# Five weight pairs, three raw buffers, ten product buffers and two units split earlier in a macaron decoder trunk

## The chip, the cores and the metric

The kernel runs on one core of a Trainium2 chip. The metric is the device time of one execution in microseconds (us). The engines are PE (matmul), DVE (vector), ACT (scalar), POOL (GpSimd) and SP, which issues the weight loads. Each works through its own instructions in the order in which they stand, and they wait for each other on semaphores.

## What is computed

A decoder trunk of two layers for a sequence of 256 tokens of width 1024, in float32. Each layer is a half-weighted SwiGLU feed-forward block (FFN), a mixer and a second FFN. The mixer of layer 0 is a convolution, that of layer 1 an attention.

```python
def swiglu_ffn(x, w_gate_up, w_down):
    gate, up = jnp.split(x @ w_gate_up, 2, axis=-1)
    return (jax.nn.silu(gate) * up) @ w_down

def conv_mixers(h, w_in, a_kernel, b_kernel, b_bias, b_ln_g, b_ln_b, w_out):
    z = h @ w_in
    a_b, a_c, a_x, b_val, b_gate = jnp.split(z, [512, 1024, 1536, 2048], axis=-1)
    y_a = a_b * causal_depthwise_conv(a_c * a_x, a_kernel)          # 3 taps
    u = b_val * jax.nn.sigmoid(b_gate)
    u = causal_depthwise_conv(u, b_kernel) + b_bias                 # 31 taps
    y_b = jax.nn.silu(layer_norm(u, b_ln_g, b_ln_b))
    return jnp.concatenate([y_a, y_b], axis=-1) @ w_out
...
    for layer in range(2):
        x = x + 0.5 * swiglu_ffn(rms_norm(x, ffn1_norm[layer]), ffn1_w_gate_up[layer], ffn1_w_down[layer])
        h = rms_norm(x, mix_norm[layer])
        x = x + (conv_mixers(h, ...) if layer % 2 == 0 else dilated_attention(h, ...))
        x = x + 0.5 * swiglu_ffn(rms_norm(x, ffn2_norm[layer]), ffn2_w_gate_up[layer], ffn2_w_down[layer])
    return rms_norm(x, final_norm)
```

## The kernel before

Activations lie transposed in SBUF, 128 features by 256 tokens, as eight tiles. All weights come as one stream of 162 **units** of 1 MB (16 tiles of 128x128): units 0 to 21 are gate and up of the first FFN, 22 to 32 its down projection, 33 to 42 the ten pairs of the convolution's input projection, 43 to 46 its output projection, 47 to 79 the second FFN, and 80 to 161 layer 1 in the same way. SP loads unit by unit into the pool `raws`. `split` then writes a unit as two rounded halves, `w1` (a copy on ACT, line 127) and `w2` (the rest, a subtraction on DVE, line 128), each in two pieces of 1024 columns, or in four of 512 for the units in `FINE` (39, 46 and 47). PE multiplies with both halves (lines 163 to 165, or 169 and 170). The units in `whole` (0, 35, 42, 43 and 44) are not split: PE multiplies with the raw tile (line 161), and they keep their raw buffer until that is done.

`advance(u, ahead)` says how far the stream must be by unit `u`: units below `u + RAWS + WS - 1` are loaded, those below `u + ahead` split. `RAWS` is 4, `WS`, the number of buffers of `w1` and of `w2`, is 4 too, and `ahead` is `WS` unless it is given. In the convolution the table `AHEAD` gives it for each of the ten input units, `OUT_AHEAD` for units 43 and 44. A scheduler sets the final order on each engine from the order in the code and from priorities: `high_priority` puts a part of the code ahead of what stands before it, as for the layer norm of the convolution (`PRIO_LN`).

The convolution's stage, `conv`, is where the change works most. For each of four channel groups `c`, the 31 taps are shared: DVE adds its own into a PSUM tile (line 464), and for the others ACT multiplies (`prod`, line 486) and POOL adds (`yp`, line 487), 55 such adds in all. The products go through a pool of `PBUFS` = 18 buffers. `PER_STEP` and `PER_POOL` spread the taps over the ten units. The short convolution (`m`, then `ya`: ACT starts each group at line 518, DVE goes on at line 527) is gated by the last two units at lines 538 and 539. The sum over all channels for the layer norm goes through `sums` (line 561) into a matmul with ones (line 563), while PE multiplies the `ya` half with units 43 and 44. The normalised half, `ob`, then meets units 45 and 46; from their result come `x` (line 420) and the next block's `xs` (lines 190 and 191).

PSUM banks `pa` are four. DVE's reads at lines 382 and 340 set them free in an FFN.

Of the kernel before, what the change touches and what calls it, by code (L numbers as in the profile page):

```python
# [33 lines left out]
UT = 16  # L34
# [3 lines left out]
PER_STEP = [9, 8, 7, 8, 8, 8, 9, 8, 9, 10]  # L38
PRIO = 0
WHOLE = {9, 2}  # L40
PBUFS = 18
PER_POOL = [6, 8, 2, 6, 6, 9, 6, 4, 8, 9]
XPRIO = 0
AHEAD = [2, 4, 1, 1, 4, 4, 3, 4, 3, 3]
LATE = 15
OUT_AHEAD = [2, 3]
PRIO_LN = 800
# [18 lines left out]
M_POOL = [0, 0, 0, 0]  # L66
T_POOL = [0, 0, 0, 0]
B_POOL = [0, 0]
RAWS = 4
WS = 4  # L70
TWO = (3,)
ROBIN = False
SU_POOL = 2
# [21 lines left out]
def trunk(ctx: ExitStack, tc: tile.TileContext, xin, wst, cst, bia, idn, out):  # L95
    nc = tc.nc
    keep = ctx.enter_context(tc.tile_pool(name="keep", bufs=1))
    keep.tile([P, (LINE - BASE % LINE) // 4], F32, name="gap")
    raws = ctx.enter_context(tc.tile_pool(name="raws", bufs=RAWS))
    w1s = ctx.enter_context(tc.tile_pool(name="w1s", bufs=WS))  # L100
    w2s = ctx.enter_context(tc.tile_pool(name="w2s", bufs=WS))
    tmp = ctx.enter_context(tc.tile_pool(name="tmp", bufs=2))
# [4 lines left out]
    n_units = wst.shape[0]  # L107
    ahead_load, ahead_split = RAWS + WS - 1, WS
    raw, w1, w2 = {}, {}, {}
    at = {"load": 0, "split": 0}  # L110

    def load(u):
        raw[u] = raws.tile([P, UT * P], F32, name="raw")
        n = UT * P // PIECES.get(u, 1)
        for c in range(0, UT * P, n):
            nc.sync.dma_start(raw[u][:, c:c + n], wst[u][:, c:c + n])

    def split(u):
        if u in whole:
            return  # L120
        w1[u] = w1s.tile([P, UT * P], F32R, name="w1")
        w2[u] = w2s.tile([P, UT * P], F32R, name="w2")
        n = max(2, PIECES.get(u, 1), FINE.get(u - first_conv, 1))
        h = UT * P // n
        for i in range(n):
            c = slice(i * h, (i + 1) * h)
            nc.scalar.copy(w1[u][:, c], raw[u][:, c])  # L127
            nc.vector.tensor_sub(w2[u][:, c], raw[u][:, c], w1[u][:, c].bitcast(F32))  # L128
        del raw[u]

    def advance(u, ahead_split=ahead_split):
        while at["load"] < min(n_units, u + ahead_load):
            load(at["load"])
            at["load"] += 1
        while at["split"] < min(n_units, u + ahead_split):
            split(at["split"])
            at["split"] += 1


    first_conv = NF + NF * ND // UT  # L140
# [13 lines left out]
    def take(n):  # L154
        st = Stream(used[0])
        used[0] += n
        return st

    def mm3(o, a, b, start, stop, check=False):
        if len(a) == 1:  # L160
            nc.tensor.matmul(o, a[0], b[-1], start=start, stop=stop, skip_group_check=check)  # L161
            return
        nc.tensor.matmul(o, a[0], b[0], start=start, stop=False, skip_group_check=check)  # L163
        nc.tensor.matmul(o, a[0], b[1], start=False, stop=False, skip_group_check=check)  # L164
        nc.tensor.matmul(o, a[1], b[0], start=False, stop=stop, skip_group_check=check)  # L165

    def mm2(o, w, b, start, stop):

        nc.tensor.matmul(o, w[0], b, start=start, stop=False, skip_group_check=True)  # L169
        nc.tensor.matmul(o[:, 0], w[1], b[:, 0], start=False, stop=stop, skip_group_check=True)  # L170
# [13 lines left out]
    def split_to(o1, o2, src, scale=None):  # L184

        if scale is None:
            nc.scalar.copy(o1, src)
            nc.vector.tensor_sub(o2, src, o1.bitcast(F32))
        else:
            nc.scalar.activation(o1, src, AF.Copy, scale=scale)  # L190
            nc.vector.scalar_tensor_tensor(o2, src, scale, o1.bitcast(F32),  # L191
                                           op0=ALU.mult, op1=ALU.subtract)
# [119 lines left out]
    def twice(r):  # L312
        return r[:, None, :].to_broadcast([P, 2, S])

    def project(st, base, xs, xg=None):

        bank = psa.tile([P, 2, S], F32, name="pa")
        for i in range(2):
            for k in range(ND):
                w = st.tile(base + 2 * k + i)  # L320
                b = (xs[:, k, 0], xs[:, k, 1]) if len(w) == 2 else (xg[:, k],)
                mm3(bank[:, i], w, b, k == 0, k == ND - 1)
        return bank

    def project2(st, base, xs):

        banks = []
        for i in range(2):
            bank = psa.tile([P, 2, S], F32, name="pa")
            for k in range(ND):  # L330
                mm2(bank, st.tile(base + 2 * k + i), xs[:, k], k == 0, k == ND - 1)
            banks.append(bank)
        return banks

    def join(v, banks, r):

        for i, bank in enumerate(banks):
            h = tmp.tile([P, S], F32, name="sq")
            nc.scalar.copy(h, bank[:, 1])  # L339
            nc.vector.tensor_add(v[:, i], bank[:, 0], h)  # L340
        nc.vector.tensor_mul(v, v, twice(r))  # L341
# [23 lines left out]
    def ffn(norm, after, between=None, first=None):  # L365
        _, r = norm.end(True, first is None)
        with tc.tile_pool(name="gp", bufs=1, reuse_waits="tile") as gp:
            st = take(NF)
            start = GS_START[st.u // FFN_STEP] // 4
            gs = gp.tile([P, NF * 2 * S + start], F32R, name="gs")[:, start:].rearrange(  # L370
                "p (f t s) -> p f t s", f=NF, t=2)
            for p in range(NF):
                advance(st.u + p)
                one = p < ONES[st.u // FFN_STEP] or p >= NF - ONE_END
                if one:
                    bank = first if first and p == 0 else project(st, p * UT, norm.xs)
                else:
                    banks = project2(st, p * UT, norm.xs)
                with tc.high_priority(offset=PRIO_F):
                    v = tmp.tile([P, 2, S], F32, name="v")  # L380
                    if one:
                        nc.vector.tensor_mul(v, bank, twice(r))
                    else:
                        join(v, banks, r)
                    sl = tmp.tile([P, S], F32, name="sl")
                    nc.scalar.activation(sl, v[:, 0], AF.Silu)  # L386
                    g = tmp.tile([P, S], F32, name="g")
                    nc.vector.tensor_mul(g, sl, v[:, 1])
                    split_to(gs[:, p, 0], gs[:, p, 1], g)
            if between:  # L390
                between(gs[:, NF - 1, 0, :1].bitcast(F32))
            st = take(NF * ND // UT)
            for d in range(ND):
                acc = psb.tile([P, 2, S], F32, name="pb")
                two = d < ND - 1
                for f in range(NF):
                    t = d * NF + f
                    if t % UT == 0 or f == 0:
                        advance(st.u + t // UT)
                    if two:  # L400
                        mm2(acc, st.tile(t), gs[:, f], f == 0, f == NF - 1)
                    else:
                        mm3(acc[:, 0], st.tile(t), (gs[:, f, 0], gs[:, f, 1]), f == 0, f == NF - 1)
                for i in range(2 if two else 1):
                    nc.vector.scalar_tensor_tensor(x[:, d], acc[:, i], 0.5, x[:, d],  # L405
                                                   op0=ALU.mult, op1=ALU.add)
                after.add(d)
# [15 lines left out]
    def conv(norm, after):  # L423
        with tc.tile_pool(name="cp", bufs=1, reuse_waits="tile") as cp, \
                tc.tile_pool(name="cp2", bufs=PBUFS, reuse_waits="tile") as cp2:
            xg = cp.tile([P, ND, S], F32, name="xg")
# [65 lines left out]
            for p in range(10):  # L492
                advance(st.u + p, AHEAD[p])
                bank = project(st, p * UT, norm.xs, xg)
# [225 lines left out]
    for layer in range(DEPTH):  # L720
        nxt = Norm(C_MX + layer * ND, start=XS_START["MX"][layer])
        if layer == 0:
            ffn_first(norm, nxt)
        else:
            ffn(norm, nxt)
        norm, nxt = nxt, Norm(C_F2 + layer * ND, start=XS_START["F2"][layer])
        (conv if layer % 2 == 0 else attention)(norm, nxt)
        if layer < DEPTH - 1:
            norm, nxt = nxt, Norm(C_F1 + (layer + 1) * ND, start=XS_START["F1"][layer + 1])
            ffn(norm, nxt)  # L730
            norm = nxt
    with tc.tile_pool(name="fp", bufs=1, reuse_waits="tile") as fp:
# [4 lines left out]
        last = Norm(C_FN, y)  # L737
# [97 lines left out]
```

## Time and profile before

| what | us |
|---|---|
| median of three runs | 969.8 |
| lowest and highest run | 968.5 and 969.87 |
| the profiled execution, its own time | 970.47 |
| its span, first to last instruction | 968.7 |
| PE busy | 953.3 |
| DVE busy | 738.5 |
| ACT busy | 557.8 |
| POOL busy, all within the convolution and just behind it | 47.9 |

The profiled execution lies 0.7 us above the median. A busy time says how long an engine had an instruction at work; matmuls are pipelined, so two neighbours overlap in the records. Where a row ends with a bracket, it gives the idle time of the engine just before and what ended it. Times are counted from the span's start.

### The profile page before, as it was taken

To read this page: it belongs to the slowest core of one execution; us is meant where nothing else is said; L and a number is where in the kernel's file an instruction comes from. 1 tells how busy PE (TensorE), PEld (TensorE's weight loads), DVE (VectorE), ACT (ScalarE), POOL (GpSimd) and SP (SyncE) were. 2 spreads that over 40 slices of the span, in tenths; PEclk is the share of its full clock that TensorE was granted. 3 is DMA by queue.
4 is the path that set the end of the run, shared out by engine and by line. 5 is a ranking of instruction groups with operands and counts; after the bars stand their busy time and mean duration, and the time that the engine had idled before them with its cause. 6 is when DMAs were issued, how large, how long until landed. Compare 5 with 4: busy or idle time off the path is not lost.

```text
span 968.7 us, 15285 instructions
## 1 busy us (share of the span) xinstructions
PE 953.3 (98%) x5876; PEld 854.3 (88%) x5876; DVE 738.5 (76%) x1401; ACT 557.8 (58%) x1019; POOL 47.9 (5%) x61
## 2 busy tenths in 40 slices
PE   8999999999899999999999999999999999999996
PEld 8988898999798888988988889898888998889886
DVE  7977776688999878766787877666799798778552
ACT  6666554488366566544456565444677566565540
POOL 0000000039600000000000000000000000000000
PEclk9999999999899999999999999999999999999998
DMA  8855555444165555555455555555553455555501
GB/s 329 286 190 201 174 189 203 174 157 149 44 261 180 211 198 194 181 198 187 174 182 210 174 193 200 179 205 202 183 190 129 134 177 211 181 209 176 195 24 44
DMA packets 27289, 176.27 MB, mean 182 GB/s; under 512 B 3024, under 2 KB 3792, under 8 KB 6864
## 3 DMA queue, kind: packets, MB, share of 16 engines
q1 hardware_dynamic: 26784, 174.67, 51.7%
q8 instruction: 46, 0.75, 0.3%
q10 hardware_dynamic: 432, 0.63, 0.2%
q14 instruction: 27, 0.22, 0.1%
HBM read 174.23 MB, written 1.05 MB: 181 GB/s over the span
## 4 chain that ended last, share of the span: by engine, by line
PE 92%; DVE 3%; ACT 2%; POOL 1%; issue 1%; DMA 1%; SPq 0%; DVEq 0%; POOLq 0%; ACTq 0%
PE pa L169 33%; PE pa L170 17%; PE pb L169 15%; PE pb L170 8%; PE pa L165 4%; PE pa L163 4%; PE pa L164 4%; PE pa L161 2%; ACT prod L486 1%; DVE pb L464 1%; PE pb L164 1%; PE pb L163 1%; PE pb L165 1%; POOL yp L487 1%; DVE w L128 1%
## 5 line engine op out<-in xcount | busy, mean ns | idle before, releaser
L169 PE MATMUL pa<-xs,w 128*128 128x512 f32 x1376 | 480.8, 394 | 0.0
L128 DVE TENSOR_TENSOR w<-raw,w 128x1024 fp32r<-128x1024 f32 (+1 forms) x322 | 381.2, 1195 | 126.8 <-ACT w L127 126.1
L127 ACT CAST w<-raw 128x1024 fp32r<-128x1024 f32 (+1 forms) x322 | 325.0, 1027 | 132.5 <-PE pa L169 50.5
L170 PE MATMUL pa<-xs,w 128*128 128x256 f32 x1376 | 385.7, 280 | 0.0
L169 PEld LDWEIGHTS pa<-xs,w 128*128 128x128 f32 x1376 | 258.3, 188 | 58.0 <-DVE xs L191 0.5
L170 PEld LDWEIGHTS pa<-xs,w 128*128 128x128 f32 x1376 | 259.6, 189 | 0.1
L169 PE MATMUL pb<-gs,w 128*128 128x512 f32 x616 | 214.8, 392 | 0.0
L170 PE MATMUL pb<-gs,w 128*128 128x256 f32 x616 | 173.5, 282 | 0.0
L169 PEld LDWEIGHTS pb<-gs,w 128*128 128x128 f32 x616 | 115.7, 188 | 25.2
L170 PEld LDWEIGHTS pb<-gs,w 128*128 128x128 f32 x616 | 116.4, 189 | 0.0
L386 ACT ACTIVATE sl<-v 128x256 f32<-128x256 f32 x88 | 36.8, 419 | 106.3 <-DVE v L341 101.3
L339 ACT COPY sq<-pa 128x256 f32<-128x256 f32 x172 | 63.3, 369 | 30.4 <-PE pa L170 25.1
L164 PE MATMUL pa<-xs,w 128*128 128x256 f32 x272 | 76.5, 282 | 0.1
L163 PE MATMUL pa<-xs,w 128*128 128x256 f32 x272 | 76.5, 283 | 0.0
L165 PE MATMUL pa<-xs,w 128*128 128x256 f32 x272 | 76.4, 281 | 0.0
L340 DVE TENSOR_TENSOR v<-pa,sq 128x256 f32<-128x256 f32 x156 | 64.9, 416 | 0.0
L405 DVE SCALAR_TENSOR_TENSOR x<-pb,x 128x256 f32<-128x256 f32 x60 | 25.3, 422 | 43.0 <-PE pb L170 29.1
L487 POOL TENSOR_TENSOR yp<-yp,prod 128x256 f32<-128x256 f32 x55 | 46.2, 843 | 211.3 <-ACT prod L486 207.3
L190 ACT ACTIVATE xs<-x,const 128x256 fp32r<-128x256 f32 x48 | 24.2, 505 | 56.5 <-DVE x L405 43.2
L341 DVE TENSOR_TENSOR v<-v,rr 128x512 f32<-128x512 f32 x78 | 53.2, 683 | 0.0
L164 PEld LDWEIGHTS pa<-xs,w 128*128 128x128 f32 x272 | 51.8, 190 | 0.5 <-DVE xs L191 0.3
L165 PEld LDWEIGHTS pa<-xs,w 128*128 128x128 f32 x272 | 51.4, 189 | 0.4 <-DVE w L128 0.4
(176 smaller groups left out, 980.8 us busy)
## 6 DMA issues: line engine op xcount, KB each, us to landing
raw<-wst SPq DMA_DIRECT2D x159, 1024.0 KB, 4.8
bt<-bia SPq DMA_DIRECT2D x8, 384.0 KB, 3.3
raw<-wst SPq DMA_DIRECT2D x7, 256.0 KB, 6.3
raw<-wst SPq DMA_DIRECT2D x2, 512.0 KB, 5.6
x<-xin SPq DMA_DIRECT2D x3, 256.0 KB, 6.1
out<-y SPq DMA_DIRECT2D x2, 256.0 KB, 2.5
out<-y ACTq DMA_DIRECT2D x2, 256.0 KB, 2.4
x<-xin SPq DMA_DIRECT2D x2, 128.0 KB, 2.9
```

The costliest lines, as they stand in the source:

```text
L127: nc.scalar.copy(w1[u][:, c], raw[u][:, c])
L128: nc.vector.tensor_sub(w2[u][:, c], raw[u][:, c], w1[u][:, c].bitcast(F32))
L163: nc.tensor.matmul(o, a[0], b[0], start=start, stop=False, skip_group_check=check)
L164: nc.tensor.matmul(o, a[0], b[1], start=False, stop=False, skip_group_check=check)
L165: nc.tensor.matmul(o, a[1], b[0], start=False, stop=stop, skip_group_check=check)
L169: nc.tensor.matmul(o, w[0], b, start=start, stop=False, skip_group_check=True)
L170: nc.tensor.matmul(o[:, 0], w[1], b[:, 0], start=False, stop=stop, skip_group_check=True)
L339: nc.scalar.copy(h, bank[:, 1])
L340: nc.vector.tensor_add(v[:, i], bank[:, 0], h)
L341: nc.vector.tensor_mul(v, v, twice(r))
L386: nc.scalar.activation(sl, v[:, 0], AF.Silu)
L487: nc.gpsimd.tensor_add(yp[:, c], yp[:, c], t)
```

## The change

Five pairs of `w1` and `w2` buffers stand in place of four, three raw buffers in place of four, and ten product buffers in place of 18; the memory of the three together stays the same. The load distance `RAWS + WS - 1` stays seven units, and wherever `ahead` isn't given, splits run one unit further ahead. At the last unit of the FFN before the convolution (unit 32) `advance` is called with `WS + 1`, so units up to 37 are split there; before, 36 and 37 were split in the convolution. `AHEAD` follows suit.

```diff
-PBUFS = 18
+PBUFS = 10
...
-AHEAD = [2, 4, 1, 1, 4, 4, 3, 4, 3, 3]
+AHEAD = [5, 1, 4, 4, 4, 4, 3, 4, 3, 3]
...
-RAWS = 4
-WS = 4
+RAWS = 3
+WS = 5
...
                     if t % UT == 0 or f == 0:
-                        advance(st.u + t // UT)
+                        last = st.u + t // UT == first_conv - 1
+                        advance(st.u + t // UT, WS + 1 if last else WS)
```

From line 399 on, the lines of the changed kernel are numbered one higher. The scheduler makes another order of it. Three places are shown, each with the kernel before first and the changed one second.

ACT, from the copies for unit 41 (`w`, last unit to be split in the convolution) to the end of the convolution. `prod` are the products for POOL, `yp` the first tap of a group, `ya` the start of a short convolution.

```order
L127 CAST w_2453<-raw 128x1024 x2
L518 ACTIVATE ya<-m,const 128x256
L486 ACTIVATE prod<-u,const 128x256 x6
L481 ACTIVATE yp<-u,const 128x256
L486 ACTIVATE prod<-u,const 128x256 x15
L518 ACTIVATE ya<-m,const 128x256 x2
L127 CAST w_2848<-raw 128x1024 x2
L518 ACTIVATE ya<-m,const 128x256
```

```order
L127 CAST w_2453<-raw 128x1024
L487 ACTIVATE prod<-u,const 128x256
L482 ACTIVATE yp<-u,const 128x256
L487 ACTIVATE prod<-u,const 128x256 x12
L519 ACTIVATE ya<-m,const 128x256
L482 ACTIVATE yp<-u,const 128x256
L487 ACTIVATE prod<-u,const 128x256 x15
L519 ACTIVATE ya<-m,const 128x256 x3
```

The first `ya` now stands behind six more products, the other three stand behind all 55, and the copies of unit 45 (`w_2848`) have left their place between them.

PE, from unit 42 (`xg`, the last input unit, 16 matmuls with a whole weight) to the end of units 43 and 44 (`ya`). The matmul `pb<-sums,ones` takes the layer norm's sum.

```order
L161 MATMUL pa<-xg,raw 128x256 x16
L161 MATMUL pa<-ya,raw 128x256 x4
L563 MATMUL pb<-sums,ones 128x256
L161 MATMUL pa<-ya,raw 128x256 x12
L201 MATMUL pb<-ones,sums 128x2 x2
L161 MATMUL pa<-ya,raw 128x256 x9
L241 MATMUL pb<-ident,wide 128x128 x2
L161 MATMUL pa<-ya,raw 128x256 x7
```

```order
L161 MATMUL pa<-xg,raw 128x256 x13
L564 MATMUL pb<-sums,ones 128x256
L161 MATMUL pa<-xg,raw 128x256 x3
L161 MATMUL pa<-ya,raw 128x256 x7
L201 MATMUL pb<-ones,sums 128x2 x2
L161 MATMUL pa<-ya,raw 128x256 x6
L241 MATMUL pb<-ident,wide 128x128 x2
L161 MATMUL pa<-ya,raw 128x256 x19
```

The sum's matmul has moved from behind four `ya` products to ahead of the last three matmuls of unit 42.

DVE, from the second half of the convolution's output (`ob`) to the first `xs` of the second FFN. Of the pairs `w`, units 47 and 48 are `w_2958` and `w_2968` in both kernels, unit 46 is `w_2855` in the changed one; the kernel before has split it further up.

```order
L188 TENSOR_TENSOR ob_2035<-sl,ob_2034 128x256 x2
L128 TENSOR_TENSOR w_2958<-raw,w_2957 128x512
L128 TENSOR_TENSOR w_2968<-raw,w_2967 128x1024
L188 TENSOR_TENSOR ob_2035<-sl,ob_2034 128x256 x2
L128 TENSOR_TENSOR w_2968<-raw,w_2967 128x1024
L420 TENSOR_TENSOR x<-pa,x 128x256 x3
L191 SCALAR_TENSOR_TENSOR xs<-x,const,xs 128x256 x2
```

```order
L188 TENSOR_TENSOR ob_2047<-sl,ob_2046 128x256 x4
L128 TENSOR_TENSOR w_2855<-raw,w_2854 128x512 x4
L421 TENSOR_TENSOR x<-pa,x 128x256
L128 TENSOR_TENSOR w_2958<-raw,w_2957 128x512 x4
L191 SCALAR_TENSOR_TENSOR xs<-x,const,xs 128x256
L421 TENSOR_TENSOR x<-pa,x 128x256 x3
L128 TENSOR_TENSOR w_2968<-raw,w_2967 128x1024 x2
L191 SCALAR_TENSOR_TENSOR xs<-x,const,xs 128x256
```

All of units 46, 47 and 48 now stands behind `ob` and among the first `x` and `xs`; units 49 and 50 follow between the next ones.

## Rows read from the trace of the kernel before

**Rows 1.** The page: busy us, share of the span and instructions by engine

```profile
PE 953.3 (98%) x5876; PEld 854.3 (88%) x5876; DVE 738.5 (76%) x1401; ACT 557.8 (58%) x1019; POOL 47.9 (5%) x61
```

**Rows 2.** Waits of PE: for whom, us in total, times, longest

```profile
PE pa L161 <- DVE ya L539: 3.7, 1, 3.7
PE pa L353 <- DMA raw<-wst: 1.8, 1, 1.8
```

**Rows 3.** PE in order of time: start, us, line, operation, records, idle before

```profile
248.56 7.07 PE L161 MATMUL pa<-xg,raw 128*128 128x256 f32 x32
259.35 3.78 PE L161 MATMUL pa<-ya,raw 128*128 128x256 f32 x8 [3.71 <-DVE ya L539]
262.92 1.06 PE L563 MATMUL pb<-sums,ones 128*128 128x256 f32 x2
...
277.23 0.83 PE L163 MATMUL pa<-ob,w 128*128 128x256 f32 x4
...
294.89 0.78 PE L169 MATMUL pa<-xs,w 128*128 128x512 f32 x2
```

**Rows 4.** Stretches: length; busy PE, PEld, DVE, ACT, POOL; granted clock; DMA; GB/s

```profile
259.30:265.10 5.80, 5.75 (x14) 4.59 (x15) 5.19 (x12) 0.62 (x2) 0.73 (x1) 0.50 0.07 31
265.10:277.20 12.10, 12.10 (x61) 10.76 (x60) 10.46 (x42) 7.27 (x16) 0.00 (x0) 1.00 0.70 261
```

**Rows 5.** DVE in order of time, from its wait to the layer norm's sum

```profile
243.98 0.93 DVE L527 SCALAR_TENSOR_TENSOR ya<-m,const,ya 128x256 f32<-128x256 f32 x1 [4.29 <-ACT ya L518]
...
260.60 0.68 DVE L538 TENSOR_TENSOR v<-pa,rr 128x512 f32<-128x512 f32 x1
261.25 0.42 DVE L561 TENSOR_TENSOR sums<-sums,y 128x256 f32<-128x256 f32 x1
```

**Rows 6.** ACT in order of time, its last product and the `ya` behind it

```profile
243.04 0.51 ACT L486 ACTIVATE prod<-u,const 128x256 f32<-128x256 f32 x1 [0.30 <-POOL yp L487]
243.45 0.49 ACT L518 ACTIVATE ya<-m,const 128x256 f32<-128x256 f32 x1
```

**Rows 7.** POOL's adds: the timeline, then groups of 239 to 244 and 223 to 228

```profile
207.71 50.24 POOL L487 TENSOR_TENSOR yp<-yp,prod 128x256 f32<-128x256 f32 x55 [207.27 <-ACT prod L486]
...
L487 POOL TENSOR_TENSOR yp<-yp,prod 128x256 f32<-128x256 f32 x7 | 5.2, 736 | 0.5
...
L487 POOL TENSOR_TENSOR yp<-yp,prod 128x256 f32<-128x256 f32 x4 | 4.8, 1191 | 0.3
```

**Rows 8.** The page's groups, DVE's splits: busy us, mean ns, idle before

```profile
L128 DVE TENSOR_TENSOR w<-raw,w 128x1024 fp32r<-128x1024 f32 (+1 forms) x322 | 381.2, 1195 | 126.8 <-ACT w L127 126.1
```

**Rows 9.** The stretch of the first FFN, columns as in rows 4

```profile
60.00:195.00 135.00, 135.00 (x810) 119.88 (x809) 95.45 (x144) 71.95 (x116) 0.00 (x0) 1.00 0.54 189
```

**Rows 10.** DVE in order of time, the read of a fourth bank in the first FFN

```profile
37.21 0.68 DVE L382 TENSOR_TENSOR v<-pa,rr 128x512 f32<-128x512 f32 x1
```

**Rows 11.** PE in order of time, the first matmuls of two banks that follow each other

```profile
40.43 0.40 PE L169 MATMUL pa<-xs,w 128*128 128x512 f32 x1
...
43.26 0.40 PE L169 MATMUL pa<-xs,w 128*128 128x512 f32 x1
```

**Rows 12.** SP in order of time, the issues of the loads of units 46 and 47

```profile
255.67 0.33 SPq L116 DMA_DIRECT2D raw<-wst  x1
266.97 0.33 SPq L116 DMA_DIRECT2D raw<-wst  x1
```

**Rows 13.** The page's loads: count, KB each, median us from issue to landing

```profile
raw<-wst SPq DMA_DIRECT2D x159, 1024.0 KB, 4.8
```

**Rows 14.** DVE in order of time, before and at the second FFN's start

```profile
275.92 1.28 DVE L128 TENSOR_TENSOR w<-raw,w 128x512 fp32r<-128x512 f32 x2
...
293.50 1.23 DVE L128 TENSOR_TENSOR w<-raw,w 128x1024 fp32r<-128x1024 f32 x1 [0.54 <-ACT w L127]
294.64 0.48 DVE L191 SCALAR_TENSOR_TENSOR xs<-x,const,xs 128x256 fp32r<-128x256 f32 x1
295.04 0.42 DVE L300 TENSOR_TENSOR sums<-sums,sq 128x256 f32<-128x256 f32 x1
```

## The prediction

> **What bounds the kernel now.** The busy times come first: PE is busy for 953 of 968.7 us [rows 1], so a change on another engine can gain only where PE stands still. The list of PE's waits starts with 3.7 us on a DVE write of `ya` and 1.8 us on the first load [rows 2]. Only the first of them lies where the change works. PE's order in time shows its place [rows 3]: unit 42, the last convolution projection, runs from 248.56, and the first output product with `ya` starts at 259.35. The table by stretches then shows a second price of that wait: from 259.3 to 265.1 the granted clock is 0.50, the 1.2 GHz level, after PE stood still for 3.7 us, and it is 1.00 again behind that [rows 4]. Half a clock for 5.8 us is 2.9 us of matmul time. So wait and clock together, 6.6 us, are all that can be won there, and the rest of the span is matmuls back to back.
>
> Why is `ya` late? DVE stood still for 4.29 us until 243.98, waiting for a `ya` of ACT (line 518) [rows 5]. ACT wrote it at 243.45, directly behind its 55th and last product at 243.04 [rows 6]. ACT could not write that product earlier, since POOL adds the products one by one for 50.24 us without a pause [rows 7] and only 18 may wait for it. Counting back checks it: POOL's last add ends at 257.95, 18 adds at 0.81 (0.736 busy and 0.07 to the next, from the group of seven) earlier is 243.4, and the row says 243.04. So the convolution hangs on POOL, with the product buffers as the string between POOL and the rest.
>
> **The change part by part: two units split earlier.** Units 36 and 37 lose their place in the convolution: four half-unit subtractions on DVE at 1.195 [rows 8], about 4.6 us with the overlap of neighbours, and four copies on ACT. In the FFN before, DVE is busy for 95 of 135 us and PE for all of them [rows 9], so they fit into DVE's idle time there and cost nothing; without that room they would cost their 4.6. Unit 39, cut in four, also moves ahead of the first product. POOL's own gain: four adds that ran beside two half-unit splits averaged 1.191 instead of 0.736 to 0.74 [rows 7], so such a half costs POOL 0.45 x 4 / 2 = 0.9. The whole stretch is 50.24 - 55 x 0.81 = 5.6; four halves (3.6) stay under POOL, four quarters of unit 39 leave, and with 0.6 for smaller writes POOL ends near 207.7 + 44.6 + 4.2 = 256.5, 1.4 earlier than now.
>
> The row shows POOL slowed and not stopped for the whole DVE instruction. The Trainium skill (SBUF — State Buffer, SBUF: two separate sides) says that a DVE instruction with two SBUF inputs and a GpSimd instruction exclude each other for the whole instruction; by that, a half would cost POOL its full 1.2, and POOL would end 1.2 later than in my sum. The sum takes the measured 0.9.
>
> **Ten product buffers.** The 55th product of the changed kernel needs the buffer of the 45th, so ACT writes it when POOL is through with add 45: 256.5 - 10 x 0.81 = 248.4. In the new order on ACT three `ya` (line 519) stand behind all 55 products, as now. The first of them starts 0.41 later as now, at 248.8, and DVE's waiting instruction 0.53 behind that [rows 5, 6], at 249.3; today it is 243.98. So the two units taken off DVE buy nothing: DVE only waits longer for ACT, which waits for POOL. What DVE has queued behind that wait is the rest of the taps, the second half of the gated products and the sum `sums` for the layer norm: today from 243.98 to 261.67 [rows 5], 17.7 us. In the new order one multiply (0.65) and one add (0.33) stand elsewhere and one multiply with a tap (0.73) comes in: 17.4. The sum is then ready at 266.7, five microseconds later than now.
>
> **The layer norm's matmul stands earlier in PE's order.** The scheduler has put it (line 564) ahead of the last three of unit 42's 16 matmuls. Today four `ya` products come before it. PE works through its queue in order, so everything behind it waits. Thirteen of the 16 at 0.42 (7.07 for 32 records) are done at 254.0; the wait is 266.8 - 254.0 = 12.8 us in place of 3.7. Behind it come 35 whole-weight matmuls, where today 28 follow. Today it takes from 262.92 to 277.23 [rows 3], 14.3 us, 2.2 of them at half clock, so 13.2 at full clock; seven more make 16.1, and 5.8 us at half clock, which I take as today from PE's restart [rows 4], add 2.9. PE gets to unit 45 at 266.8 + 19.0 = 285.8 instead of 277.2: **8.6 us**. The norm's own chain took 14.3 today beside this and stays hidden under 19.0. The ends of this term: with no stretch on POOL at all it is 4.2 less, 4.4; if POOL stood still for the whole 1.195 of each half [rows 8], 1.2 more, 9.8.
>
> **Three raw buffers.** Units 42, 43 and 44 are multiplied unsplit out of their raw buffers, so they occupy all three until PE is through with each. Today a fourth lets unit 46 load at 255.67 and 47 at 266.97 [rows 12], long before the FFN. In the changed kernel 46 loads when 43 is done: 266.8 + 0.8 + 21 matmuls at 0.42 + 0.9 for the norm's small ones + 2.9 for the clock = 280.2, lands 4.8 later [rows 13] at 285.0, and after one ACT quarter DVE starts on it at 285.5. Then DVE has, in its new order, eight quarters (two in 1.28, 0.60 each), seven halves (1.14 from start to start), eight `x` (0.34), eight `xs` (0.40) and six sums (0.34, each starting 0.08 before its neighbour ends) up to the last `xs` [rows 14]: 4.8 + 8.0 + 2.7 + 3.2 + 2.0 = 20.7, to 306.2. PE, from 285.8, would finish units 45 to 47 at 5.66 each (a bank of eight pairs takes 2.83 [rows 11]) at 302.8 and wants that `xs` at 302.5. Today the same `xs` ends at 295.12, in the midst of PE's last step of unit 47 at 294.89 [rows 3, 14], so there is no slack left to lose. I take **3.5 us**, and 0 to 5 as its ends: the lower if PE can go on with unit 48's first bank meanwhile, the upper if loads land as late as two in a row.
>
> **Five pairs.** In a running FFN nothing waits today, and one more unit in advance gives PE nothing. At the start, though, one more unit is split ahead of the first reads of PE's banks: two halves, 2.3 us on DVE. The read of the fourth bank ends today at 37.9, and PE wants it again at 40.43 [rows 10, 11]: 2.5 us of cover. I take 0, and 2.3 as the upper end, should that cover be gone.
>
> **Sum.** 8.6 + 3.5 + 0 = 12.1 us. The profiled execution took 970.47 with a span of 968.7, so 982.6; the median of the runs is 969.8, 0.7 below it, which makes 981.9. I predict **982 us**.
>
> **The rivals.** (a) *Only the wait at the norm grows.* PE's order has some freedom between units 46 and 48, and the late `xs` may be covered: 969.8 + 8.6 = 978.4. For it: the load is only two units late; against it: today's slack of nothing. The Trainium skill (Trainium Kernel Development and Optimization, Best Practices) asks for double buffering to overlap loads with work, by which three raw buffers are plenty; here three are taken by whole weights, which that rule does not count. Chance 0.15. (b) *The change does what it looks like: faster.* If ACT does not hold DVE, the 4.6 us taken off DVE exceed the wait of 3.7; the wait and its half clock go, and the time is 969.8 - 6.6 = 963.2. It decides at DVE's wait for `ya`: ACT's last product must come before DVE gets there at 239.7 [rows 5], and with ten buffers POOL would have to be through with 45 adds by then, which are 36.5 us from 207.7 even with no stretch, 244.2. Against it stands the unbroken POOL row. Chance 0.06. (c) *Gain and loss cancel*, if POOL runs unstretched, the late `xs` is covered and the half clock falls away: 4.4 - 2.9 = 1.5, so 971.3, chance 0.03. (d) *Worse*: 2.3 at the start, POOL still for whole halves (1.2) and 1.5 more at the second FFN: 987. Chance 0.08. My forecast has 0.68.
>
> **How the numbers follow.** Slower by over 0.2% (1.9 us, about what a measurement of this kernel can tell from no change) is forecast, (a), (d) and most of what lies between them and (c): 0.91. Same 0.03, faster 0.06. The range runs from 976, (a) with a POOL term a little under its middle, to 987, (d); below it lie (b), (c) and the lowest part of (a).
>
> **What would show it.** Right: one PE wait of about 12 us on `sums` at line 564, half clock for some 6 us behind it, POOL ending near 256 to 257, more waits of ACT's products for POOL than today, DVE's last wait for `ya` ending near 249, and in the first units of the second FFN PE waits for `xs` of 3 to 4 us together. Wrong: PE reaching line 564 without a wait, DVE resuming before 245, or loads of units 46 and 47 issued before PE has left unit 43. New waits of PE in the first 50 us would show the start's term.

## The result and the profile after

The changed kernel takes 982.1 us (median of four runs, 979.7 to 985.4) against 969.6 for the kernel before: a ratio of 1.0133, interval 1.0102 to 1.0165. Run again with the experiments, on another occasion, it took 983.4 us, 1.0139 (1.0125 to 1.0154). The forecast was 982 us, with the range 976 to 987. The profiled execution took 979.7, with a span of 977.7; it is the lowest of the four, 2.4 below their median; a second profile, among the experiments, shows where such a difference comes from.

The busy times, in the order of [rows 1]:

```profile
PE 952.0 (97%) x5876; PEld 853.4 (87%) x5876; DVE 737.9 (75%) x1401; ACT 560.4 (57%) x1019; POOL 46.1 (5%) x61
```

No engine has more instructions than before, and only ACT is busy longer, by 2.6 us; PE is even busy 1.3 us less while the span is 9.0 longer. So the time is in waits. PE's waits, in the columns of [rows 2] (us in total, times, longest):

```profile
PE pb L564 <- DVE sums L562: 11.9, 1, 11.9
...
PE pa L353 <- DVE xg L349: 1.2, 1, 1.2
PE pa L169 <- ACT w L127: 1.2, 1, 1.2
PE pa L169 <- DVE xs L191: 1.1, 2, 0.9
...
PE pa L169 <- DVE v L340: 0.3, 1, 0.3
```

The wait of 3.7 for `ya` is gone, and one of 11.9 for `sums` stands in its place. Three small ones at line 169 are new: two at the second FFN's start (`w` and `xs`), one in the first FFN (`v`). PE in order of time shows the places (start, us, ..., idle before):

```profile
247.16 5.77 PE L161 MATMUL pa<-xg,raw 128*128 128x256 f32 x26
264.81 1.22 PE L564 MATMUL pb<-sums,ones 128*128 128x256 f32 x2 [11.89 <-DVE sums L562]
265.82 2.77 PE L161 MATMUL pa<-xg,raw 128*128 128x256 f32 x6
...
283.03 0.47 PE L163 MATMUL pa<-ob,w 128*128 128x256 f32 x1
...
295.73 0.47 PE L169 MATMUL pa<-xs,w 128*128 128x512 f32 x1 [1.24 <-ACT w L127]
...
299.70 0.50 PE L169 MATMUL pa<-xs,w 128*128 128x512 f32 x1 [0.90 <-DVE xs L191]
```

Thirteen matmuls of unit 42 run, then PE stands still with three of them still to do (the row of six records behind the wait). From unit 42's start to unit 45's take 35.87 us here, 28.67 before [rows 3]. The stretches of this wait and behind it, columns as in [rows 4]:

```profile
259.30:264.80 5.50, 0.00 (x0) 0.00 (x0) 4.89 (x12) 0.00 (x0) 0.72 (x1) 0.50 0.00 0
264.80:268.50 3.70, 3.69 (x9) 2.97 (x10) 1.75 (x5) 1.49 (x4) 0.00 (x0) 0.50 0.02 4
268.70:283.00 14.30, 14.30 (x71) 12.59 (x70) 9.54 (x39) 6.07 (x12) 0.00 (x0) 1.00 0.54 192
```

The clock was at its 1.2 GHz level in the last 5.5 us of PE's wait, stayed there for 3.7 us of its work, and rose. Now the chain that holds the sum: POOL's adds, ACT's last product and the `ya` behind it, DVE's wait for that `ya`, and the sum (compare [rows 5 to 7]):

```profile
206.27 48.52 POOL L488 TENSOR_TENSOR yp<-yp,prod 128x256 f32<-128x256 f32 x55 [205.83 <-ACT prod L487]
...
246.54 0.51 ACT L487 ACTIVATE prod<-u,const 128x256 f32<-128x256 f32 x1 [0.30 <-POOL yp L488]
246.95 0.49 ACT L519 ACTIVATE ya<-m,const 128x256 f32<-128x256 f32 x1
...
247.48 0.92 DVE L528 SCALAR_TENSOR_TENSOR ya<-m,const,ya 128x256 f32<-128x256 f32 x1 [6.21 <-ACT ya L519]
...
264.33 0.42 DVE L562 TENSOR_TENSOR sums<-sums,y 128x256 f32<-128x256 f32 x1 [0.57 <-POOL sums L562]
```

The last product starts 8.25 us ahead of POOL's end at 254.79, ten adds of 0.82. DVE runs out of other work at 241.3 and stands still for 6.21; before, it was 4.29 until 243.98. Last, the loads of units 46 and 47 on SP, and DVE's first quarter of unit 46 and last `xs` (compare [rows 12, 14]):

```profile
277.37 1.28 SPq L116 DMA_DIRECT2D raw<-wst  x2
...
282.96 0.69 DVE L128 TENSOR_TENSOR w<-raw,w 128x512 fp32r<-128x512 f32 x1 [2.12 <-ACT w L127]
...
304.84 0.48 DVE L191 SCALAR_TENSOR_TENSOR xs<-x,const,xs 128x256 fp32r<-128x256 f32 x1
```

Unit 46 was issued at 255.67 before and is at 277.37 now, when PE is through with unit 43's 16 products; unit 47 follows a microsecond later in the buffer that unit 45's split has left.

### The profile page after: what moved, and what is told of

Its sections match the earlier page's. It is cut to its first block, busy times and chain, and to the rows that moved or that the text cites. A ratio compares the mean times of both kernels' runs of the same rounds, so it can differ in the third digit from the quotient of the medians.

```text
span 977.7 us, 15299 instructions
## 1 busy us (share of the span) xinstructions
PE 952.0 (97%) x5876; PEld 853.4 (87%) x5876; DVE 737.9 (75%) x1401; ACT 560.4 (57%) x1019; POOL 46.1 (5%) x61
## 4 chain that ended last, share of the span: by engine, by line
PE 89%; DVE 4%; POOL 4%; ACT 1%; DMA 1%; issue 1%; SPq 0%; POOLq 0%; DVEq 0%; ACTq 0%
PE pa L169 31%; PE pa L170 16%; PE pb L169 14%; PE pb L170 8%; PE pa L165 4%; PE pa L163 4%; POOL yp L488 4%; PE pa L164 4%; PE pb L164 1%; PE pb L163 1%; PE pb L165 1%; DVE w L128 1%; PE pa L161 1%; DVE pb L465 1%; PE pb L666 1%
## 5 line engine op out<-in xcount | busy, mean ns | idle before, releaser
L190 ACT ACTIVATE xs<-x,const 128x256 fp32r<-128x256 f32 x48 | 24.3, 506 | 53.9 <-DVE x L406 43.2
```

## The experiments

For all of them PE's way is cut at three points that each profile has: PE's first matmul of unit 42, its first of unit 45 (with `ob`), and DVE's read of a bank in the second FFN that stands at 320.26 before. The table gives what each stretch takes more or less than before (A up to unit 42, 248.56 before; B from there to unit 45, 28.67; C to the read, 43.03; D to the end, 648.4), how long PE worked at half clock within B, and the medians in us. The sum of A to D is the difference of the spans of one profile; the ratio is that of the runs.

| run | A | B | C | D | half clock in B | median, ratio (interval) |
|---|---|---|---|---|---|---|
| before | 0 | 0 | 0 | 0 | 5.8 | 969.5 to 970.0 |
| after | -1.4 | +7.2 | +4.1 | -1.0 | 3.7 | 982.1, 1.0133 (1.0102 to 1.0165) |
| after, second profile | -1.1 | +7.7 | +4.8 | +1.0 | 4.5 | 983.4, 1.0139 (1.0125 to 1.0154) |
| before, 10 product buffers | -0.7 | +6.0 | 0.0 | +0.1 | 5.9 | 975.1, 1.0060 (1.0048 to 1.0072) |
| before, three raw buffers | -0.4 | -1.1 | +2.2 | +0.1 | 3.4 | 972.5, 1.0029 (1.0019 to 1.0039) |
| after, 18 product buffers | +0.5 | +1.9 | +4.2 | +1.5 | 4.1 | 978.4, 1.0088 (1.0075 to 1.0101) |
| before, `ya` on DVE | +0.3 | -4.1 | +0.5 | -0.5 | 0 | 967.3, 0.9980 (0.9972 to 0.9988) |
| after, norm's matmul later | -0.2 | +5.4 | +6.2 | +1.0 | 3.8 | 982.3, 1.0124 (1.0109 to 1.0138) |
| after, `ya` on DVE | -1.1 | -0.1 | +6.4 | +1.1 | 3.4 | 976.4, 1.0062 (1.0046 to 1.0079) |
| after, 18 buffers and matmul later | -1.5 | +0.4 | +4.3 | -0.9 | 5.9 | 974.2, 1.0047 (1.0034 to 1.0060) |
| before, one unit split earlier in the code alone | -0.5 | -1.0 | +0.4 | +0.7 | 3.4 | 969.1, 0.9996 (0.9987 to 1.0004) |
| the same, `ya` on DVE | -0.9 | -2.9 | +0.6 | -0.5 | 0 | 967.1, 0.9979 (0.9970 to 0.9988) |

**Product buffers alone.**

```diff
-PBUFS = 18
+PBUFS = 10
```

> The kernel before with one edit: 10 product buffers in place of 18. Theory (product buffers hold ACT, ACT holds the ya that DVE waits for): ACT's last product comes 10 adds of 0.81 us ahead of POOL's end instead of 18, so about 6.5 us later (249.5 instead of 243.0), DVE resumes near 250.4, PE's wait for the gated ya grows from 3.7 to about 10 us, the start of the second FFN loses nothing: 976 us. Rival 1 (the loss of the changed kernel comes from raw buffers and order, the product buffers are idle): 969.6 us, PE's wait stays 3.7. Rival 2 (the product buffers are the whole loss): 982 us.

PE's one long wait, and ACT's last product with the `ya` behind it:

```profile
PE pa L161 <- DVE ya L539: 9.7, 1, 9.7
```

```profile
248.72 0.51 ACT L486 ACTIVATE prod<-u,const 128x256 f32<-128x256 f32 x1 [0.29 <-POOL yp L487]
249.13 0.50 ACT L518 ACTIVATE ya<-m,const 128x256 f32<-128x256 f32 x1
```

The order on PE, DVE, ACT and POOL is that of the kernel before. The last product comes 5.7 us later than at 243.04 [rows 6], PE's wait grows by 6.0, and nothing else moves: stretch B carries it all. Measured 975.1 for an expected 976. Both rivals fall: the buffers are not idle, and they are not the whole loss.

**Raw buffers alone.**

```diff
-RAWS = 4
+RAWS = 3
```

> The kernel before with one edit: three raw buffers in place of four (the load distance falls from seven units to six with it). Theory: the convolution stays as it is (PE's wait 3.7 us, POOL's end near 258), unit 46 loads only when unit 43 is multiplied, near 270 instead of 255.7, and the second FFN starts late by 3 us (1.5 to 5): 972.6 us. Rival 1 (the late loads are covered by work of PE that comes first): 969.6 us. Rival 2 (load distance matters everywhere, waits of PE in each FFN): over 976 us.

PE's waits that differ from [rows 2], and SP's issues for unit 46 and the next:

```profile
PE pa L161 <- DVE ya L539: 3.7, 1, 3.7
...
PE pa L169 <- DVE xs L191: 0.9, 1, 0.9
```

```profile
268.68 1.76 SPq L116 DMA_DIRECT2D raw<-wst  x2
```

The convolution's wait is untouched, unit 46 is issued 13 us later than at 255.67 [rows 12], and PE waits for an `xs` in the second FFN; stretch C is 2.2 longer and the time 2.5. This is the theory, and the rival by which PE's other work covers the late loads falls. The edit also takes the load distance from seven units to six, which the changed kernel keeps at seven; the run doesn't tell these two apart. In this profile the -1.1 in B hides part of it: behind the same wait of 3.7 PE had 3.4 us at half clock instead of 5.8.

**The changed kernel with 18 product buffers.**

```diff
-PBUFS = 10
+PBUFS = 18
```

> The changed kernel with 18 product buffers again, the rest as changed. Theory: ACT's last product is no longer held by the buffers, DVE resumes near 242.5 instead of 247.5, the sum for the layer norm is ready near 260, PE's wait at its matmul falls from 11.9 to about 6 to 7 us, the late loads at the second FFN stay: 977 us. Rival (the matmul's early place and the raw buffers carry the loss): 982 us, wait still 11 to 12 us.

PE's waits of this run in the convolution and at the second FFN's start:

```profile
PE pb L564 <- DVE sums L562: 6.4, 1, 6.4
PE pa L169 <- DVE xs L191: 2.3, 3, 1.2
```

The wait falls to the 6 to 7 us expected, the time to 978.4 (977 expected). The loss at the second FFN stays at 4.2. One thing asks for more: the norm's matmul now runs 12.2 us behind unit 42's start (261.17 against 249.02), earlier than the 14.4 of before [rows 3], and still stretch B is 1.9 longer. Behind it come seven more matmuls than before, which points to its early place.

**The start of `ya` on DVE, in the kernel before.**

```diff
-                        nc.scalar.activation(ya[:, c], m[:, c, :S], AF.Copy,
-                                             scale=const[:, ka:ka + 1])
+                        nc.vector.tensor_scalar_mul(ya[:, c], m[:, c, :S],
+                                                    const[:, ka:ka + 1])
```

> The kernel before with the start of the short convolution (ya) on DVE in place of ACT; all sizes as before. Theory (what costs time is that ya stands behind ACT's products, which wait for POOL): DVE no longer stands still for 4.3 us near 240, it takes on four multiplications of about 0.45 us, the gated ya are ready some 2.5 us earlier, PE's wait falls from 3.7 to under 1.5 us and the half clock behind it goes: 964 us. Rival (DVE itself is the bound of this stage, the wait was only slack): 970 to 971 us.

PE's waits for `ya`, DVE's new operation, and the stretch from unit 42 on:

```profile
PE pa L161 <- DVE ya L539: 2.0, 2, 1.6
```

```profile
239.45 0.62 DVE L518 TENSOR_SCALAR ya<-m,const 128x256 f32<-128x256 f32 x1
```

```profile
247.00:275.00 28.00, 25.63 (x132) 22.05 (x131) 25.73 (x77) 8.84 (x20) 11.82 (x16) 1.00 0.42 152
```

All sizes are as before, and the `ya` no longer stands behind ACT's products; the scheduler has also put the norm's matmul behind seven `ya` products where it stood behind four. DVE's wait near 240 is gone, PE's falls to 2.0 in two pieces, and the clock stays at 1.00. B is 4.1 shorter. The time is 967.3, below both kernels; 964 was expected, since I took 1.5 us for the waits that are 2.0 and 2.9 us of half clock that other runs of the kernel before don't always have. The rival, DVE as the bound, falls.

**The changed kernel once more.**

> The changed kernel once more, unedited. Theory (its profiled execution was 3 us below its median because a pair of matmuls took 0.347 us in the first FFN where the kernel before took 0.353, and because stretches at half clock differ from run to run): the waits come back within 0.3 us (11.9 at the layer norm's matmul, 2.3 in the second FFN's first units), while the span may be 978 to 983, with the pair at 0.347 or 0.353: 982 us. Rival (the quicker pairs belong to the changed order): 0.347 again in the first FFN.

The same two waits of PE in the second profile:

```profile
PE pb L564 <- DVE sums L562: 12.0, 1, 12.0
PE pa L169 <- DVE xs L191: 3.1, 3, 1.2
```

The wait at the norm's matmul comes back within 0.1 us; those of the second FFN are 3.1 us in place of 2.3, more than the 0.3 allowed. The span is 981.1 where it was 977.7, the difference being +0.3 in A, +0.5 in B, +0.7 in C and +2.0 in D. The quick pair of matmuls was there again in the first FFN, as the rival said. Most of D is the same effect in the second FFN (last section).

**The norm's matmul behind two `ya` products.** In the changed kernel the priority of that one matmul is cut from 800 to 40, so that it stands behind unit 42's last three matmuls and two `ya` products.

```diff
-                pm = psb.tile([P, S], F32, name="pb")
-                nc.tensor.matmul(pm, ones, su, start=True, stop=True)
+            with tc.high_priority(offset=40):
+                pm = psb.tile([P, S], F32, name="pb")
+                nc.tensor.matmul(pm, ones, su, start=True, stop=True)
+            with tc.high_priority(offset=PRIO_LN):
                 sq2 = tmp.tile([P, S], F32, name="sums")
```

> The changed kernel with the layer norm's first matmul behind unit 42's last three matmuls and two ya products, where the changed kernel has it ahead of all five. Theory (PE stands at that matmul although other work is ready): the gated ya are ready near 262.3, some 2.5 us ahead of the sum, so PE's one wait of 11.9 becomes one of 8 to 8.5 for ya and one of about 1 for the sum, PE gets to unit 45 2 to 3 us earlier: 979.5 us. Rival (the place costs nothing, PE waits for the sum either way): 982 us.

PE's waits of this run (line 565 is the norm's matmul here), and a stretch of its second FFN with the columns of [rows 4]:

```profile
PE pa L161 <- DVE ya L540: 9.6, 1, 9.6
PE pa L169 <- DVE xs L191: 3.3, 2, 2.1
...
PE pb L565 <- DVE sums L562: 0.3, 1, 0.3
```

```profile
299.90:303.20 3.30, 3.30 (x13) 2.90 (x13) 2.23 (x7) 1.52 (x4) 0.00 (x0) 0.50 0.79 305
```

Up to unit 45 the theory holds: PE waits 9.9 in place of 11.9 to 12.0 and B is 1.8 to 2.3 shorter. But the time, 982.3, can't be told from the changed kernel's. The gain is given back at the second FFN. Unit 46 is issued earlier, at 275.46 instead of 277.37, but DVE has its `ob` to do until 282.2 and starts on the unit's first quarter at 282.25 instead of 282.96; the fifth `xs` starts at 299.11 instead of 299.18. One of PE's waits there grows to 2.1, and now the clock falls to half there too (the last row), 1.7 us of matmul time that the changed kernel doesn't lose.

**The start of `ya` on DVE, in the changed kernel** (the diff of the fourth run).

> The changed kernel, 10 product buffers included, with the start of ya on DVE in place of ACT. Theory (the product buffers cost time only because ya stands behind ACT's products): DVE no longer waits 6.2 us, the sum is ready near 258 instead of 264.7, PE's wait at the layer norm's matmul falls from 11.9 to 2 to 5 us, the loss at the second FFN (3.8) stays: 973 us. Rival (POOL or DVE holds the sum anyway): 978 us or more.

PE's waits of this run at the norm's matmul and in the second FFN:

```profile
PE pb L564 <- DVE sums L562: 4.7, 1, 4.7
PE pa L169 <- DVE xs L191: 1.9, 2, 1.0
...
PE pa L169 <- DVE x L421: 1.5, 1, 1.5
```

With ten product buffers still in place, B is about that of the kernel before (-0.1, with 2.4 us less at half clock, which is 1.2). ACT still waits 10.9 us for POOL in its products, but DVE no longer waits for a `ya`, and the sum follows POOL's own last add: most of what the buffers cost comes from `ya` standing behind the products. The edit isn't clean, since the scheduler has put the norm's matmul behind all 16 matmuls of unit 42 here, where 13 stood before it; three matmuls are 1.3 us of the 7.2 that the wait lost. The time is 976.4 instead of 973, since C is 2 us worse than in the changed kernel: again half clock in the second FFN (3.3 us at 293.4), and a new wait in the first (0.7 us).

**18 product buffers and the matmul later**, the two edits together.

> The changed kernel with 18 product buffers and with the layer norm's first matmul behind unit 42 and two ya products (both edits of the two runs before together). Theory (matmul's place and product buffers are the whole loss of the convolution, 4 to 5 us of 978.4 hang on the place once the buffers are back): 974 us, the rest above 970 being the second FFN's start. Rival (five pairs or the earlier splits cost the convolution something of their own): 977 to 978 us.

PE's waits of this run, and the stretch in which its clock was at half:

```profile
PE pa L169 <- DVE xs L191: 2.9, 2, 1.7
PE pa L161 <- DVE ya L540: 2.4, 1, 2.4
...
PE pb L565 <- DVE sums L562: 1.3, 1, 1.3
```

```profile
258.10:264.80 6.70, 5.91 (x14) 4.75 (x15) 4.31 (x10) 3.38 (x6) 0.27 (x1) 0.50 0.01 5
```

974.2 for an expected 974. The convolution is as long as before (+0.4), what is left is the second FFN's start (+4.3). So buffers and place are the convolution's whole loss; five pairs and the earlier splits, taken together, neither cost nor gain there. Between this run and that with 18 buffers alone the medians differ by 4.2, the stretches B by only 1.5. Here PE had 1.8 us more at half clock, which is 0.9, and the run with 18 buffers had the slower pair of matmuls in both FFNs in its one profile; how much of the 4.2 the place is worth from run to run stays open.

**One unit split earlier in the code, all sizes as before**, first alone and then with `ya` on DVE. Four pairs let one unit, 36, be split at the last unit of the FFN.

```diff
-AHEAD = [2, 4, 1, 1, 4, 4, 3, 4, 3, 3]
+AHEAD = [4, 1, 1, 1, 4, 4, 3, 4, 3, 3]
...
-                        advance(st.u + t // UT)
+                        last = st.u + t // UT == first_conv - 1
+                        advance(st.u + t // UT, WS + 1 if last else WS)
```

> The kernel before with its own four pairs, four raw buffers and 18 product buffers, and one unit (36) split earlier, in the FFN ahead of the convolution; two units don't fit into four pairs. Theory (the wait belongs to ACT's ya behind POOL's adds, so DVE work taken out of the convolution only lengthens DVE's wait, and POOL gains the 1.8 us at most that two half splits cost it): PE's wait falls from 3.7 to between 3.7 and 2.5, 969 us (968 to 970). Rival (an earlier split pays off as such, 2.4 us of DVE and the half clock): 965 us.

> The run before with ya's start on DVE too, that is the kernel of the fourth run (967.3 us) with unit 36 split earlier. Theory: with ACT out of the chain DVE and POOL are the bound, both are relieved, PE's two waits of 2.0 together fall to about 1.5: 966.8 us. Rival (POOL's 55 adds alone are the bound): 967.3 us, the same waits.

Neither run moves a split. The order of the instructions on PE, DVE, ACT and POOL comes out as in the kernel before, and with `ya` on DVE as in the run that has that edit alone. Unit 36 stood ahead of the convolution already. DVE's two halves of it and PE's first matmul of the convolution, in the kernel before and then in the run with the split alone:

```profile
190.47 2.36 DVE L128 TENSOR_TENSOR w<-raw,w 128x1024 fp32r<-128x1024 f32 x2 [0.78 <-ACT w L127]
194.91 0.28 PE L163 MATMUL pa<-xs,w 128*128 128x256 f32 x1
```

```profile
190.01 2.36 DVE L128 TENSOR_TENSOR w<-raw,w 128x1024 fp32r<-128x1024 f32 x2 [0.78 <-ACT w L127]
194.44 0.28 PE L163 MATMUL pa<-xs,w 128*128 128x256 f32 x1
```

So the two are repeats of the kernel before (969.1 against 969.5 us) and of that run (967.1 against 967.3). What an earlier split is worth by itself stays untested, and neither the theories nor the rivals are decided. As repeats they show the spread. The -1.0 in B of the first is half clock, 3.4 us instead of 5.8, behind a wait of 3.8. In the second PE waits 3.3 us for `ya` instead of 2.0: it came to unit 42 1.2 us earlier, while POOL's adds ended at 258.5 in the one and 258.4 in the other.

**A wait made in the first FFN.** DVE's read of the two banks of the fifth pair is done twice, and in the next run three times, the same sum into the same place.

```diff
-            nc.vector.tensor_add(v[:, i], bank[:, 0], h)
+            for _ in range(times):
+                nc.vector.tensor_add(v[:, i], bank[:, 0], h)
...
-                        join(v, banks, r)
+                        join(v, banks, r, 2 if st.u == 0 and p == 4 else 1)
```

> The kernel before with one edit in the first FFN: at its fifth pair of gate and up DVE's read of each of the two banks is done twice, the same sum into the same place, so that PE gets the next bank about 0.5 us late, as it does in the changed kernel near 43 us. Theory (a short standstill of PE lets the pair of matmuls go over from 0.353 to 0.347 us for the rest of the FFN): one PE wait of 0.2 to 0.6 us near 43, 0.347 behind it, unit 42 reached 1 us earlier: 969.1 us. Rival (the quicker pairs come with the five pairs' places in memory): 0.353 stays, 970.3 us.

> The run before with the reads of the two banks done three times each in place of twice, which had left PE without any wait near 43 us. Theory (a short standstill of PE lets the pair of matmuls go over from 0.353 to 0.347 us): one PE wait of 0.5 to 1.5 us near 44, 0.347 behind it up to 130, and about 969.3 us, the wait paid back by 1.4. Rival (the quicker pairs come with the five pairs' places in memory): 0.353 stays and the time is 970.5 to 971.

Twice gave no wait of PE near 43 us (969.6 us, 1.0000, 0.9992 to 1.0009): inconclusive. Three times gave one, and the group of PE's long matmuls from 60 to 125 us (count, busy us, mean ns) shows what came behind it:

```profile
PE pa L169 <- DVE v L341: 0.8, 1, 0.8
```

```profile
L169 PE MATMUL pa<-xs,w 128*128 128x512 f32 x185 | 65.4, 399 | 0.0
```

The mean is 399 ns as in the kernel before; 969.4 us, 0.9993 (0.9984 to 1.0001). So a standstill alone does not bring the quicker pair.

## Why the prediction held, point by point

**What bounds the kernel.** PE's wait and its half clock, DVE behind ACT's `ya`, ACT behind POOL: shown by two runs. Fewer product buffers, with the order on every engine unchanged, lengthened PE's wait by 6.0 us; `ya` taken off ACT cut it to 2.0 us and took the half clock away (967.3).

**Two units earlier.** "Buy nothing" held, but no run shows it by itself, and the four halves were two. Unit 36 was split ahead of the convolution in the kernel before too (the row above); of the two units only 37 stood in it, its halves at 196.1 and 201.3. With 18 product buffers in the changed kernel DVE waited 5.5 us for `ya`, 4.3 in the kernel before, which fits work taken off DVE turning into wait; with the matmul's place mended too, the convolution was as long as before (+0.4). POOL took 48.5 us (48.6 in the second profile) for the 48.8 of the sum: four half-unit splits stayed under it and unit 39's quarters left. By the rule of the Trainium skill (SBUF — State Buffer, SBUF: two separate sides) the prediction's estimate comes to 50.0; the measurement is on the side of the partial slowdown.

**Ten product buffers.** The last product came ten adds ahead of POOL's end, as reckoned; DVE resumed at 247.5 instead of 249.3, and 1.4 of that is the earlier start of the whole stage. DVE's tail from there to the sum was 17.3 (17.4).

**The matmul's place: 8.6 forecast, 7.2 and 7.7 measured.** The mechanism held, two sizes were off. The wait was 11.9 instead of 12.8: the sum came 0.55 earlier against unit 42's start, and thirteen matmuls took 0.33 longer than I had. And the half clock lasted 3.7 and 4.5 us of PE's work where I had carried over 5.8 from [rows 4], 0.7 to 1.0 us of time. That was the mis-sized term: 5.8 was one draw, not a constant. The term holds the ten buffers as well as the place, since the sum comes late by them. The runs part the two: the buffers made 6.0 alone, and giving them back took off 5.3 to 5.8; the place made 1.8 to 2.3, or 1.5 with 18 buffers.

**Three raw buffers: 3.5 forecast, 4.1 and 4.8 measured at the second FFN**, within the term's ends of 0 and 5. Unit 46 was issued at 277.4, when 43 was through, as reckoned (280.2, less 1.4 for the earlier stage and 1.4 for wait and clock). DVE then took 22.4 us to the last `xs` instead of 20.7, with waits for ACT and PE of 1.3 us in between that I had not counted; that was mis-sized. But the raw buffers are not the whole of it. From PE's first matmul of unit 45 to the end of the last `xs` it is 17.9 us in the kernel before, 20.4 with three raw buffers alone, 22.3 and 22.9 in the changed kernel. DVE's half-unit splits in that stretch, with three raw buffers alone and in the changed kernel:

```profile
L128 DVE TENSOR_TENSOR w<-raw,w 128x1024 fp32r<-128x1024 f32 x5 | 6.0, 1220 | 0.6 <-ACT w L127 0.5
```

```profile
L128 DVE TENSOR_TENSOR w<-raw,w 128x1024 fp32r<-128x1024 f32 x7 | 8.3, 1216 | 0.5 <-ACT w L127 0.5
```

The two halves more are the one unit further ahead that five pairs bring: 2.3 us of DVE's time in front of the `xs`. The sum counted all seven halves, but under the name of the raw buffers. The run with 18 buffers and the matmul later bears this out: it issues unit 46 7.0 us ahead of unit 45's start, as the run with three raw buffers alone does, has seven halves, and its last `xs` ends at 22.4. No run has five pairs with four raw buffers, so this sharing out is read from rows and not shown by an edit. Alone, three raw buffers cost 2.5 us. The rival (a), with double buffering as the Trainium skill asks for it (Trainium Kernel Development and Optimization, Best Practices) behind it, falls with that run: the spare buffers were held by unsplit weights.

**Five pairs: 0 forecast, 0.6 measured at the start**, besides their share at the second FFN. DVE's read of the fourth bank starts at 39.12 instead of 37.21, although the whole began 0.6 earlier: 2.5 us of delay on the 2.5 us of cover that I had found [rows 10, 11]. So the cover was used up. PE waited 0.3 us for a bank and started it at 43.22, where it was 43.26 before: its lead of 0.6 was gone.

**What the sum did not have.** A start 0.6 us earlier, a pair of matmuls that ran quicker in the first FFN (about -1.5), and slower in the second in one profile and not in the other. The spans of the two profiles are 9.0 and 12.4 above the kernel before, the medians 12.5 and 13.4, and 12.1 was forecast; of the 3.4 between the profiles some 1.9 are this pair's pace in the second FFN and 0.4 the half clock. That the forecast fits the first median to 0.1 us is partly luck: the term of the matmul's place was 0.9 to 1.4 too large, those of the second FFN and of the start too small, and the pair's pace was not in it.

**The rivals.** (b), faster, needed ACT out of DVE's way: with `ya` on DVE this happens with the sizes of before (967.3), not by this change. (c) and (d) have no part in it.

## What to carry to other kernels

Before a pool of buffers is cut, find out what stands in the same queue behind the operation that fills it: here eight product buffers were worth 5 us mainly because four small multiplications stood behind the products on ACT, and in the changed kernel moving these gained more (976.4) than giving the buffers back (978.4). Count the buffers of a pool that are held by work that doesn't release them early (whole weights), since only the rest overlaps loads. Work taken off an engine that waits for another may only make it wait longer. And before a run is read as a test of an edit, compare the order on each engine: an edit to the code's order can leave it as it was, and an edit to one operation can move another.

## What was not expected of the hardware

**Two paces of the same matmuls.** The pair of lines 169 and 170 took 0.353 us or 0.347, at a granted clock of 1.00 in both. In the first FFN's gate and up the kernel before kept to 0.353; the changed kernel began with it and went over to 0.347 right behind its wait of 0.3 us at 43.2. The long matmul's group in the changed kernel from 31.5 to 39.5 us, from 60 to 125 us, and from 330 to 410 us in its first and its second profile (the kernel before has 399 ns in the second of these stretches, as in the row above):

```profile
L169 PE MATMUL pa<-xs,w 128*128 128x512 f32 x24 | 8.5, 399 | 0.0
...
L169 PE MATMUL pa<-xs,w 128*128 128x512 f32 x188 | 65.2, 394 | 0.0
...
L169 PE MATMUL pa<-xs,w 128*128 128x512 f32 x231 | 80.1, 391 | 0.0
```

```profile
L169 PE MATMUL pa<-xs,w 128*128 128x512 f32 x227 | 80.2, 399 | 0.0
```

In that stage all eight profiles with four pairs of buffers kept 0.353, and five of six with five pairs went over behind that wait. The sixth, with 18 product buffers, had the wait too (0.3 us at 43.7) and stayed at 0.353. The first FFN's down projection (150 to 185 us) ran at 0.347 in all fourteen; in the second FFN both paces came with either number of pairs. It moves the time by about 1.5 us in the first FFN and by about 1.9 in the second. Neither a standstill alone (the sixth profile, and the run with the reads done three times) nor the five pairs' places in memory alone (the sixth profile) decides it. The cause is open.

**Half clock of different length behind the same wait.** After a wait of 3.7 to 3.8 us PE worked 5.8 us at half clock in the kernel before, and 3.4 with three raw buffers and in the repeat of the kernel before; after 12 us 3.7 and 4.5, twice the same kernel; after two waits of 1.6 us and less, none. The Trainium skill (TensorE: Matmul & The Clock Gate, What's actually happening) says that the clock is decided in windows that run freely and don't begin with the kernel; the spread here agrees with it.
